# Grouped-query attention heads: two key tiles merged by predicate, four transposes a head, and value differences

## The chip, the cores and the metric

The kernel runs on one core of one Trainium2 chip. The metric is the device time of one execution in microseconds (us). Engine names follow the profile: PE is TensorE's matmuls, PEld its weight loads, DVE is VectorE, ACT is ScalarE, POOL is GpSimd, SP is the engine that issues the DMAs.

## The reference

One layer of a hybrid trunk on x of 512 tokens by 2048 channels, all float32: RMS norm, one input projection, three token mixers (A: dilated attention, 8 heads; B: a convolution module; C: sliding-window attention, 16 query heads on 2 key/value heads, 64 wide), an output projection with a residual, and a SwiGLU block with a residual. The change is in mixer C:

```python
cq = _rms_norm(cq.reshape(B, S, C_Q_HEADS, HEAD_DIM), c_q_g[l])
ck = _rms_norm(ck.reshape(B, S, C_KV_HEADS, HEAD_DIM), c_k_g[l])
cv = cv.reshape(B, S, C_KV_HEADS, HEAD_DIM)
out_c, _ = _band_attention(cq, ck, cv, C_WINDOW - 1, sinks=c_sinks[l])
```

`_band_attention` lets query t see the keys t-127 to t, takes exp(s - m), adds exp(sink - m) to the sum, multiplies by v and divides by the sum. The window is 128, so each query sees exactly 128 keys (fewer for the first 127 queries).

## The kernel before, in words

Activations lie transposed, channels on partitions and the 512 tokens as columns. Every float32 product is made of float32r parts, high and low: `mm3` (L311 to L314) issues high x high, high x low and low x high into one PSUM bank.

The program is written out in the order in which it is to run. `project` (L477) makes one 128-channel tile of the input projection by 48 matmuls 512 columns wide; after every six of them a tick is counted, and functions that are due at that tick append their instructions to the queues of their engines. `PROJ` (L47) is the order of the tiles: cv and ck early, then the q tiles of C, each with two heads, mixed with tiles for B and A. So the work of C's heads stands on PE between matmuls of the projections, and on DVE between weight splits (L290) and convolution taps (L513), from about 110 to 385 us of the span.

For one C head, `attention` (L715) cuts the 512 queries into four tiles of 128. Query tile i sees keys of tile i (the later keys, up to the diagonal) and of tile i-1 (the earlier keys, above the diagonal): a triangle of each. The steps, by `C_TICKS` (L43):

- `scores(u)`, L729: two units of two query tiles, each in one PSUM bank, 256 columns per query tile (tile 0 has 128 keys, beside which its low parts stand).
- `top(u)`, L741: DVE adds the mask bias_c to the whole 256 columns and takes the maximum, one instruction for each query tile (L750).
- `exps(u)`, L757: ACT takes the exponential of 256 columns, with the sum (L763); tile 0 has 128.
- `norm(u)`, L768: DVE makes the reciprocal of the sum, POOL multiplies the 256 columns by it (L779).
- `flip(t)`, L790: PE transposes the 128x128 blocks of the weights, seven for a head, four in the first PSUM bank and three in the second (`TBANKS`, L708).
- `high(t)` and `low(t)`, L799 and L804: ACT copies a bank to float32r (tile ph), DVE subtracts it (tile pl, L806).
- `weigh()`, L808: for each of four key tiles j, PE multiplies the values of j (high and low side by side as 128 columns) by ph and by pl: eight matmuls, six 256 wide and two 128 wide (L819, L820), into one bank, which `out_high` and `out_rows` add up.

When each step is due is worked out at the end of `attention`: `at_v` (L839) is the tick of `weigh` after that of the first scores, 18 before the change. The next head follows six ticks later. `do_v` (L679) transposes the values of the two key/value heads once, and splits them into high and low parts. `slot` (L145) takes a tile of 512 columns out of a pool of 67.

Of the kernel before, what the change touches and what calls it, by code (L numbers as in the profile page):

```python
# [15 lines left out]
P = 128  # L16
# [25 lines left out]

C_TICKS = (1, 6, 2, 2, 2, 2, 4, 1, 3)  # L43
A_TICKS = (0, 7, 2, 1, 3, 1, 3, 1, 2)
# [78 lines left out]
def kernel(ctx: ExitStack, tc: tile.TileContext, xT, wi, wo, wgu, wd, cst_in, outT):  # L123
# [253 lines left out]
    bias_a = slot("bias_a")  # L377
    bias_c = slot("bias_c", cols=2 * P)
    gqk = cp.tile([P, 2], F32, name="gqk")
# [3 lines left out]
    di2 = slot("di2", I32)  # L383
    nc.gpsimd.iota(di2[:, :2 * P], pattern=[[-1, 2 * P]], base=P, channel_multiplier=1)

    def masks():
# [9 lines left out]
        nc.vector.tensor_scalar(bias_a, mult_a, 0.0, BIG, op0=ALU.is_equal, op1=ALU.mult)  # L396
        nc.vector.tensor_copy(df[:, :2 * P], di2[:, :2 * P])
        nc.vector.tensor_scalar(r[:, :2 * P], df[:, :2 * P], 127.0, None, op0=ALU.is_le)
        nc.vector.scalar_tensor_tensor(r[:, :2 * P], df[:, :2 * P], 0.0, r[:, :2 * P], op0=ALU.is_ge, op1=ALU.mult)
        nc.vector.tensor_scalar(bias_c, r[:, :2 * P], 0.0, BIG, op0=ALU.is_equal, op1=ALU.mult)  # L400
        for i in range(2):
# [277 lines left out]
    def do_v(box, b, name):  # L679
        vs = slot(name + "s")  # L680
        nc.vector.tensor_mul(vs, b, r1b)

        def flip():
            b2 = bank(name + "t")
            for i in range(NT):
                nc.tensor.transpose(b2[:, i * P:(i + 1) * P], vs[:, i * P:(i + 1) * P], ident)
            ticks.after(1, high, b2.rearrange("p (a b c) -> p a b c", a=NT, b=2))

        def high(src):
            box["v"] = [slot(f"{name}{h}", F32R).rearrange("p (a b c) -> p a b c", a=NT, b=2) for h in range(2)]  # L690
            for h in range(2):
                nc.scalar.copy(box["v"][h][:, :, h], src[:, :, h])
            ticks.after(1, low, src)

        def low(src):
            for h, v in enumerate(box["v"]):
                nc.vector.tensor_sub(v[:, :, 1 - h], src[:, :, h], v[:, :, h].bitcast(F32))

        box["v at"] = ticks.now + VD + 3
        ticks.after(VD, flip)  # L700
# [14 lines left out]
    def attention(kind, box, mix, mi, heads):  # L715
        ready, every, step, s1, sx, s2, fl, ev, we = C_TICKS if kind == "c" else A_TICKS
        name = mi
        us = UNITS[kind]
        mask = bias_c if kind == "c" else bias_a
        mw = mask.shape[-1]  # L720
        st = {}

        def head(h):
# [17 lines left out]
            def top(u):  # L741
                b, rq = banks[u], box["rq"]
                s = slice(us[u][0][0], us[u][-1][0] + 1)
                if kind == "c" and u == 0:
                    with_kl = slot(f"kl{h}", F32, P)
                    nc.scalar.copy(with_kl, b[:, P:2 * P])
                    nc.vector.tensor_add(with_kl, with_kl, mask[:, mw - P:])
                for i, k0, n, o in reversed(us[u]):
                    other = with_kl if kind == "c" and i == 0 else mask[:, mw - n:]
                    nc.vector.tensor_tensor_reduce(b[:, o:o + n], b[:, o:o + n], other,  # L750
                                                   op0=ALU.add, op1=ALU.max, scale=1.0, scalar=-3.0e38,
                                                   accum_out=mx[:, i:i + 1])
# [4 lines left out]
            def exps(u):  # L757
                b, rq = banks.pop(u), box["rq"]
                e = es[u] = slot(f"{name}e{h}{u}")
                s = slice(us[u][0][0], us[u][-1][0] + 1)  # L760
                for i, k0, n, o in us[u]:
                    acc = dict(accum_out=den[:, i:i + 1]) if kind == "c" else {}
                    nc.scalar.activation(e[:, o:o + n], b[:, o:o + n], AF.Exp, bias=nm[:, i:i + 1],  # L763
                                         scale=rq[:, i, h:h + 1], **acc)
                if kind == "c":
                    nc.scalar.activation(mx[:, s], nm[:, s], AF.Exp, bias=col(C_SINK + heads[h]))

            def norm(u):  # L768
# [8 lines left out]
                nc.vector.reciprocal(rd[:, s], den[:, s])  # L777
                for i, k0, n, o in us[u]:
                    nc.gpsimd.tensor_scalar(e[:, o:o + n], e[:, o:o + n], rd[:, i:i + 1], None, op0=ALU.mult)  # L779

            ph, pl = {}, {}

            def block(i, j):
                for u, un in enumerate(us):
                    for ii, k0, n, o in un:
# [18 lines left out]
            def low(t, b, o):  # L804
                pl[t] = slot(f"{name}pl{h}{t}", F32R)
                nc.vector.tensor_sub(pl[t][:, :o], b[:, :o], ph[t][:, :o].bitcast(F32))  # L806

            def weigh():  # L808
                b = bank(f"{name}o{h}")
                vals = box["v"][h]  # L810
                first = True
                for t, tb in enumerate(TBANKS[kind]):
                    o = 0
# [216 lines left out]
    for half in range(2):  # L1030
# [33 lines left out]
    m_hi = m_lo = r1b = mult_a = bias_a = bias_c = None  # L1064

# [470 lines left out]
```

## Time and profile before

| | |
|---|---|
| median of 3 runs | 1879.44 us |
| the runs | 1879.31 to 1881.54 us |
| span of the profiled execution | 1877.5 us |
| instructions | 28557 |
| PE, DVE, ACT, POOL busy | 100%, 77%, 72%, 65% of the span |
| matmuls, each with a weight load | 9848 |
| granted TensorE clock | 1.00 |

The profile is of one execution of its own, whose time is shown as its span, from the first to the last instruction; the median of the runs is 1.9 us longer. In rows of the timeline stand the start, the duration, engine, line, operation, output<-inputs, the shape and, in brackets, an idle time before it and what ended it. A matmul's duration contains its way through the pipeline, so that following matmuls overlap. In rows by group stand the count, then after the bar the busy time in us and the mean of one in ns.

### The profile page before, as it was taken

How to read it: one execution, taken by the hardware profiler on the slowest of the kernel's cores; microseconds unless marked ns; L12 is line 12 of the kernel's file. 1: busy time of each engine (PE TensorE's matmuls, PEld its weight loads, DVE VectorE, ACT ScalarE, POOL GpSimd, SP SyncE). 2: the span in 40 equal slices, each digit the busy share in tenths (PEclk: the TensorE clock that was granted, in tenths of full speed). 3: DMA queues.
4: the chain of work that ended last, by engine and by line, in shares of the span. 5: the costliest groups of instructions: out<-in, count | busy, mean ns of one | idle time of the engine just before them, and what ended most of it. 6: DMA issues, size and time to landing. Idle time of an engine off the chain costs nothing.

```text
span 1877.5 us, 28557 instructions
## 1 busy us (share of the span) xinstructions
PE 1871.7 (100%) x9848; PEld 1609.1 (86%) x9848; DVE 1454.1 (77%) x2376; ACT 1343.7 (72%) x1883; POOL 1217.0 (65%) x812
## 2 busy tenths in 40 slices
PE   9999999999999999999999999999999999999999
PEld 7888888888888888888888888888888888888888
DVE  7578999897679777777777777777777677778887
ACT  6246655553466887888878888888888887777675
POOL 5023444362155887778878877888787767766786
PEclk9999999999999999999999999999999999999999
DMA  7333233333342354443544445344455475578984
GB/s 271 122 109 102 81 105 102 121 107 138 113 146 89 114 178 142 163 163 132 184 134 164 162 137 181 132 166 160 145 175 196 151 237 185 196 253 283 311 241 124
DMA packets 157986, 301.09 MB, mean 160 GB/s; under 512 B 29968, under 2 KB 69008, under 8 KB 157840
## 3 DMA queue, kind: packets, MB, share of 16 engines
q1 hardware_dynamic: 157696, 299.25, 48.8%
q8 instruction: 78, 1.28, 0.3%
q14 instruction: 68, 0.56, 0.1%
q10 hardware_dynamic: 144, 0.01, 0.0%
HBM read 241.27 MB, written 50.33 MB: 155 GB/s over the span
## 4 chain that ended last, share of the span: by engine, by line
PE 96%; DVE 1%; issue 1%; ACT 1%; POOL 1%; DMA 0%; SPq 0%; DVEq 0%; POOLq 0%; ACTq 0%
PE out L1125 51%; PE out L1267 16%; PE o L313 3%; PE o L314 3%; PE o L312 3%; PE cq L312 1%; PE cq L313 1%; PE cq L314 1%; PE in L313 1%; PE ak L312 1%; PE bg L312 1%; PE ak L314 1%; PE ak L313 1%; PE bu L312 1%; PE bu L314 1%; PE bg L313 1%
## 5 line engine op out<-in xcount | busy, mean ns | idle before, releaser
L1125 PE MATMUL out<-h,wh 128*128 128x512 f32 x2464 | 588.4, 391 | 0.0
L1125 PEld LDWEIGHTS out<-h,wh 128*128 128x128 f32 x2464 | 452.7, 188 | 87.5
L1125 PEld LDWEIGHTS out<-h,wl 128*128 128x128 f32 x2464 | 316.2, 191 | 12.4 <-DVE wl L295 0.4
L1125 PE MATMUL out<-h,wl 128*128 128x256 f32 x2464 | 320.3, 283 | 0.2 <-DVE wl L295 0.2
L1267 PE MATMUL out<-wh,a 128*128 128x512 f32 x896 | 221.3, 389 | 0.0
L1267 PEld LDWEIGHTS out<-wh,a 128*128 128x128 f32 x896 | 168.2, 188 | 34.9
L289 ACT CAST wh<-w 128x1024 fp32r<-128x1024 f32 (+1 forms) x93 | 96.7, 1042 | 125.0 <-PE o L313 43.3
L290 DVE TENSOR_TENSOR wl<-w,wh 128x1024 fp32r<-128x1024 f32 (+1 forms) x93 | 117.2, 1262 | 46.7 <-ACT wh L289 45.7
L1267 PE MATMUL out<-wl,a 128*128 128x512 f32 x448 | 119.7, 389 | 0.0
L1267 PEld LDWEIGHTS out<-wl,a 128*128 128x128 f32 x448 | 84.1, 188 | 17.4
L513 DVE SCALAR_TENSOR_TENSOR y<-bu,cst,y 128x511 f32<-128x511 f32 (+14 forms) x120 | 90.3, 753 | 0.7
L1125 PE MATMUL out<-a,wh 128*128 128x512 f32 x330 | 80.1, 391 | 0.0
L1125 PEld LDWEIGHTS out<-a,wh 128*128 128x128 f32 x330 | 60.2, 188 | 11.4
L312 PE MATMUL o<-mh_c,wh 128*128 128x512 f32 x128 | 51.2, 400 | 0.0
L313 PE MATMUL o<-ml_c,wh 128*128 128x512 f32 x128 | 50.1, 392 | 0.4 <-POOL ml_c L865 0.3
L314 PE MATMUL o<-mh_c,wl 128*128 128x512 f32 x128 | 50.1, 391 | 0.0
L1312 DVE TENSOR_TENSOR Y<-Y,out 128x512 f32<-128x512 f32 x48 | 30.8, 683 | 19.0 <-PE out L1267 18.9
L1125 PEld LDWEIGHTS out<-a,wl 128*128 128x128 f32 x330 | 43.3, 191 | 2.2
L1125 PE MATMUL out<-a,wl 128*128 128x256 f32 x330 | 44.0, 283 | 0.0
L429 POOL TENSOR_TENSOR ssum<-ssum,sq 128x512 f32<-128x512 f32 x15 | 26.6, 1770 | 19.3 <-ACT sq L428 18.8
L312 PE MATMUL cq<-hh,wh 128*128 128x512 f32 x96 | 38.6, 402 | 0.0
L314 PE MATMUL cq<-hh,wl 128*128 128x512 f32 x96 | 37.5, 391 | 0.0
(3111 smaller groups left out, 5197.0 us busy)
## 6 DMA issues: line engine op xcount, KB each, us to landing
od<-a SPq DMA_DIRECT2D x140, 256.0 KB, 4.7
a<-od SPq DMA_DIRECT2D x140, 256.0 KB, 6.2
w<-in_wi SPq DMA_DIRECT2D x59, 512.0 KB, 3.6
w<-in_wo SPq DMA_DIRECT2D x32, 512.0 KB, 3.6
x<-in_xT SPq DMA_DIRECT2D x16, 256.0 KB, 6.7
xr<-in_xT SPq DMA_DIRECT2D x16, 256.0 KB, 3.8
x2d<-xr SPq DMA_DIRECT2D x16, 256.0 KB, 2.0
yd<-z SPq DMA_DIRECT2D x16, 256.0 KB, 5.5
```

The costliest lines, as they stand in the source:

```text
L289: nc.scalar.copy(hi[:, :n], t[:, :n])
L290: eng.tensor_sub(lo[:, :n], t[:, :n], hi[:, :n].bitcast(F32))
L312: nc.tensor.matmul(out, wh, xh, start=start, stop=False)
L313: nc.tensor.matmul(out, wh, xl, start=False, stop=False)
L314: nc.tensor.matmul(out, wl, xh, start=False, stop=stop)
L429: eng.tensor_add(acc, acc, sq)
L513: nc.vector.scalar_tensor_tensor(yconv[j][:, i:], hconv[j][:, :T - i], c, yconv[j][:, i:], op0=ALU.mult, op1=ALU.add)
L1125: nc.tensor.matmul(out, lhs[:, s], rhs, start=begin, stop=last and low == flip[0] and x is xs[-1], skip_group_check=True)
L1267: nc.tensor.matmul(to[h], x[:, h * P:(h + 1) * P], v[:, j], start=sub == 0 and h not in started, stop=sub == 1 and n in (len(todo) - 1, le ...
L1312: nc.vector.tensor_add(t, t, b)
```

## The change

Since the two triangles of a query tile together are exactly 128 keys, they fit into one block: column k of the block holds the score of the later key where k is at most the query's place in the tile, and that of the earlier key elsewhere.

- `top` lays the earlier key's score over the later one's with a predicated copy on DVE (mask `earlier`, int32), one for each unit, and takes the maximum of the 128 columns with `tensor_reduce`. Query tile 0, which has no earlier tile, keeps the old way, with bias_c as a 128-column mask.
- `exps` takes 128 columns of every query tile, and all four go into one tile e; `norm` multiplies 128 columns each.
- `flip` transposes four blocks, in one bank; `high` and `low` run once a head.
- `weigh` uses p for all of a query tile's 128 keys times v of tile i, plus p of the earlier keys alone times (v of tile i-1 less v of tile i). For that `low` has POOL multiply ph and pl, 384 columns each, by the mask `later_keys` (tiles phb, plb), and `do_v` makes the differences of v (`step`, split to high and low parts, tiles cvd) once. The weighing is 4 + 4 + 3 + 3 = 14 matmuls, each 128 wide.
- The last number of `C_TICKS` goes from 3 to 5. With one bank of transposes in place of two, `at_v` goes from 18 to 19.

```diff
-C_TICKS = (1, 6, 2, 2, 2, 2, 4, 1, 3)
+C_TICKS = (1, 6, 2, 2, 2, 2, 4, 1, 5)
...
+        nc.vector.tensor_scalar(later_keys, df[:, :3 * P], 0.0, None, op0=ALU.is_gt)
+        nc.vector.tensor_scalar(bias_c, df[:, 3 * P:], 0.0, BIG, op0=ALU.is_lt, op1=ALU.mult)
+        nc.vector.tensor_scalar(earlier[:, :2 * P], df[:, :2 * P], 0.0, None, op0=ALU.is_lt)
...
+            full = slot(name + "w").rearrange("p (a b c) -> p a b c", a=NT, b=2)
+            nc.scalar.copy(full, src)
...
+            step = slot(name + "d").rearrange("p (a b c) -> p a b c", a=NT, b=2)
+            nc.vector.tensor_sub(step[:, 1:], full[:, :NT - 1], src[:, 1:])
+            ticks.after(1, step_high, step)
...
-        "c": [[(0, 0, 1), (1, 1, 2)], [(2, 2, 3), (3, 3, 3)]],
+        "c": [[(i, i, i) for i in range(NT)]],
...
+                if grouped:
+                    first = 1 - u
+                    pair = b.rearrange("p (i t k) -> p i t k", i=2, t=2)[:, first:]
+                    keys = earlier[:, :2 * P].rearrange("p (i k) -> p i k", i=2)[:, first:]
+                    nc.vector.copy_predicated(pair[:, :, 1], keys, pair[:, :, 0])
+                    nc.vector.tensor_reduce(mx[:, 2 * u + first:2 * u + 2], pair[:, :, 1],
+                                            axis=mybir.AxisListType.X, op=ALU.max)
...
+                    if grouped:
+                        src, to = b[:, o + n - P:o + n], e[:, i * P:(i + 1) * P]
...
+                if grouped:
+                    for part, p in (("h", ph), ("l", pl)):
+                        p["before"] = slot(f"{name}p{part}b{h}", F32R)
+                        nc.gpsimd.tensor_mul(p["before"][:, P:], p[t][:, P:].bitcast(F32), later_keys)
...
+                if grouped:
+                    todo = [(v, i, p[k]) for v, k, i0 in ((vals, 0, 0), (box["dv"][h], "before", 1))
+                            for p in (ph, pl) for i in range(i0, NT)]
+                    for n, (v, i, p) in enumerate(todo):
+                        s = slice(i * P, (i + 1) * P)
+                        nc.tensor.matmul(b[:, s], v[:, i].rearrange("p a b -> p (a b)"), p[:, s], start=n == 0,
+                                         stop=n == len(todo) - 1, skip_group_check=True)
```

The first place is on PE, at the weighing of the first head of c3 (c3o), before. The rows follow the projection's matmuls (cq); c3t are transposes of the second head of c3, c1s scores of c1.

```order
L314 MATMUL cq_1491<-hh_384,wl_1420 128x512
L819 MATMUL c3o_1576<-c3ph_1509,cv_831 128x256
L820 MATMUL c3o_1576<-c3pl_1527,cv_831 128x256
...
L819 MATMUL c3o_1576<-c3ph_1524,cv_831 128x128
L820 MATMUL c3o_1576<-c3pl_1541,cv_831 128x128
L795 MATMUL c3t_1585<-ident,c3e_1441 128x128 x3
L795 MATMUL c3t_1585<-ident,c3e_1481 128x128
L736 MATMUL c1s_1590<-ck_1039,cq_1487 128x256
```

The same place on PE in the changed kernel; cvd are the differences of v, phb and plb the products by `later_keys`.

```order
L314 MATMUL cq_1491<-hh_385,wl_1431 128x512
L826 MATMUL c3t_1587<-ident,c3e_1451 128x128 x4
L752 MATMUL c1s_1592<-ck_1050,cq_1487 128x256
...
L314 MATMUL cq_1491<-hh_429,wl_1431 128x512
L852 MATMUL c3o_1606<-c3ph_1519,cv_832 128x128 x4
L852 MATMUL c3o_1606<-c3pl_1535,cv_832 128x128 x4
L852 MATMUL c3o_1606<-c3phb_1537,cvd_856 128x128 x3
L852 MATMUL c3o_1606<-c3plb_1539,cvd_856 128x128 x3
L312 MATMUL cq_1491<-hh_448,wh_1430 128x512
```

The weighing has moved six projection matmuls (one tick) behind the transposes of the next head, has 14 narrow matmuls in place of eight, and the second group of transposes is gone.

The second place is POOL's queue from the second head of c0 to q of c1 (cq1r, a power), before; c3e are the weights of the two heads of c3, which are normalised here, bu is a product of mixer B.

```order
L504 TENSOR_TENSOR bu_1211<-bu_1211,bg_1340 128x512
L779 TENSOR_SCALAR c3e_1319<-c3e_1319,c3d_1062 128x128
L779 TENSOR_SCALAR c3e_1319<-c3e_1319,c3d_1062 128x256
L779 TENSOR_SCALAR c3e_1369<-c3e_1369,c3d_1062 128x256 x2
L779 TENSOR_SCALAR c3e_1441<-c3e_1441,c3d_1063 128x128
L779 TENSOR_SCALAR c3e_1441<-c3e_1441,c3d_1063 128x256
L779 TENSOR_SCALAR c3e_1481<-c3e_1481,c3d_1063 128x256 x2
L585 TENSOR_TENSOR cq1r<-cq1v,nhalf 128x8
```

The same stretch of POOL's queue in the changed kernel:

```order
L506 TENSOR_TENSOR bu_1223<-bu_1223,bg_1348 128x512
L808 TENSOR_SCALAR c3e_1327<-c3e_1327,c3d_1073 128x128 x4
L841 TENSOR_TENSOR c0phb_1426<-c0ph_1396,mask_c 128x384
L841 TENSOR_TENSOR c0plb_1428<-c0pl_1424,mask_c 128x384
L808 TENSOR_SCALAR c3e_1451<-c3e_1451,c3d_1074 128x128 x4
L841 TENSOR_TENSOR c3phb_1537<-c3ph_1519,mask_c 128x384
L841 TENSOR_TENSOR c3plb_1539<-c3pl_1535,mask_c 128x384
L587 TENSOR_TENSOR cq1r<-cq1v,nhalf 128x8
```

Two products stand in the queue for each head, behind the normalisation of the following head.

More of the change, by code (lines that the diff above doesn't have):

```diff
@@ L718, in attention @@
         us = UNITS[kind]
-        mask = bias_c if kind == "c" else bias_a
-        mw = mask.shape[-1]
+        grouped = kind == "c"
         st = {}
@@ L743, in top @@
                 s = slice(us[u][0][0], us[u][-1][0] + 1)
-                if kind == "c" and u == 0:
+                if grouped and u == 0:
                     with_kl = slot(f"kl{h}", F32, P)
                     nc.scalar.copy(with_kl, b[:, P:2 * P])
-                    nc.vector.tensor_add(with_kl, with_kl, mask[:, mw - P:])
+                    nc.vector.tensor_add(with_kl, with_kl, bias_c)
+                if grouped:
[5 more added lines that the diff above has]
+                                            axis=mybir.AxisListType.X, op=ALU.max)
                 for i, k0, n, o in reversed(us[u]):
-                    other = with_kl if kind == "c" and i == 0 else mask[:, mw - n:]
+                    if grouped and i:
+                        continue
+                    other = with_kl if grouped else bias_a[:, T - n:]
                     nc.vector.tensor_tensor_reduce(b[:, o:o + n], b[:, o:o + n], other,
```

41 lines of the change are left out of this document (27 added, 14 removed).

## Prediction

> **What bounds the kernel now.** I read the page first (shares, chain), then TensorE's waits, then the busy time of each engine in two stretches of the stage that is changed, and last the timeline of TensorE around single groups of matmuls. The page:
>
> ```profile
> span 1877.5 us, 28557 instructions
> ...
> PE 1871.7 (100%) x9848; PEld 1609.1 (86%) x9848; DVE 1454.1 (77%) x2376; ACT 1343.7 (72%) x1883; POOL 1217.0 (65%) x812
> ...
> PE 96%; DVE 1%; issue 1%; ACT 1%; POOL 1%; DMA 0%; SPq 0%; DVEq 0%; POOLq 0%; ACTq 0%
> ```
>
> TensorE is busy all the time and holds 96% of the chain that ended last. Its waits, by what it waited for:
>
> ```profile
> PE idle L409 <- DVE bones L343: 1.4, 1, 1.4
> PE o L313 <- POOL ml_c L865: 0.3, 1, 0.3
> PE c0o L820 <- DVE c0pl L806: 0.2, 1, 0.2
> ```
>
> Under a microsecond of waits lies behind the warm-up, and one of them, at c0o, is in code that changes. So two things alone can move the time: what TensorE itself has to do, and a new wait. Columns of the next rows: the stretch, its sum, then PE, PEld, DVE, ACT and POOL busy, granted clock, DMA share.
>
> ```profile
> 140.00:180.00 40.00, 39.76 (x214) 33.84 (x213) 35.48 (x88) 24.26 (x56) 12.37 (x13) 1.00 0.32 96
> 180.00:220.00 40.00, 40.00 (x212) 34.05 (x211) 37.72 (x101) 24.18 (x56) 20.77 (x19) 1.00 0.36 101
> ```
>
> The clock is granted in full. VectorE is the second engine: (40 - 35.48) + (40 - 37.72) = 6.8 us free of 80, or 8.5%. ScalarE and GpSimd have room.
>
> **What a matmul costs TensorE.** A row's duration includes the pipeline, so I use distances from start to start. One weighing (o = v x weights) of the kernel before, between projections:
>
> ```profile
> 309.42 0.39 PE L313 MATMUL bg<-hl,wh 128*128 128x512 f32 x1
> 309.64 0.39 PE L314 MATMUL bg<-hh,wl 128*128 128x512 f32 x1
> 309.87 0.28 PE L819 MATMUL c4o<-c4ph,cv 128*128 128x256 f32 x1
> ...
> 310.46 0.28 PE L820 MATMUL c4o<-c4pl,cv 128*128 128x256 f32 x1
> 310.58 0.22 PE L819 MATMUL c4o<-c4ph,cv 128*128 128x128 f32 x1
> 310.64 0.28 PE L820 MATMUL c4o<-c4pl,cv 128*128 128x128 f32 x1
> 310.76 0.45 PE L312 MATMUL bg<-hh,wh 128*128 128x512 f32 x1
> 311.04 0.39 PE L313 MATMUL bg<-hl,wh 128*128 128x512 f32 x1
> ```
>
> A 512-wide matmul takes 0.23 us (309.64 to 309.87). From 309.64 to 311.04 are 1.40 us; less two 512-wide ones (L314 and L312, 0.46) the eight matmuls of the weighing cost 0.94. Six are 256 wide: 309.87 to 310.58 is 0.71, 0.12 each. The two 128-wide ones are left with 0.94 - 0.71 = 0.23, so 0.115 each: as much as 256 columns, though the first of them is followed after 0.06. The weight loads of the same place say why:
>
> ```profile
> 310.47 0.19 PEld L819 LDWEIGHTS c4o<-c4ph,cv 128*128 128x128 f32 x1
> 310.59 0.19 PEld L820 LDWEIGHTS c4o<-c4pl,cv 128*128 128x128 f32 x1
> 310.70 0.19 PEld L312 LDWEIGHTS bg<-hh,wh 128*128 128x128 f32 x1
> 310.81 0.19 PEld L313 LDWEIGHTS bg<-hl,wh 128*128 128x128 f32 x1
> ```
>
> Every matmul has a load of its own, and they start no closer than 0.11 us, behind the 128-wide matmuls too. A matmul narrower than about 256 columns costs its load. Transposes agree:
>
> ```profile
> 160.05 0.39 PE L314 MATMUL cq<-h,wl 128*128 128x512 f32 x1
> 160.28 0.49 PE L795 MATMUL c3t<-ident,c3e 128*128 128x128 f32 x3
> 160.53 0.48 PE L312 MATMUL cq<-h,wh 128*128 128x512 f32 x1
> 160.84 0.39 PE L313 MATMUL cq<-h,wh 128*128 128x512 f32 x1
> ```
>
> 160.05 to 160.84 less 0.46 is 0.33 for three, 0.11 each.
>
> **The change on TensorE.** The order of instructions shows that it does what it says: transposes of the grouped heads fall from 112 to 64 (7 to 4 for each of 16 heads), weighing matmuls rise from 128 to 224 (8 to 14), all 128 wide, and no other matmul changes.
> - Transposes: 3 x 0.11 = 0.33 us less a head.
> - Weighing: 14 x 0.112 (between the 0.11 of the loads and the 0.115 of the pair) = 1.57 against 0.94: 0.63 more a head. With 0.11 it is 0.60, with 0.115 0.67. The columns that stream are the same, 14 x 128 = 1,792; what grows is the number of weight loads.
> - Sum: +0.30 a head (0.27 to 0.34), 16 heads: **+4.8 us** (4.3 to 5.4). It all lies on the path, since TensorE has no idle time to hide it.
>
> Here a rule of the Trainium skill speaks the other way. Its page "TensorE: Matmul & The Clock Gate", section "Back-to-back issue gap", gives about 81 ns sustained for a matmul of 128 columns with its load. By that figure a weighing would be 14 x 0.081 = 1.13, +0.19 a head, and the sum (0.19 - 0.33) x 16 = -2.2 us, faster. The same section's 131 ns for 512 columns is not what this trace has (0.23), so I hold to the rows.
>
> **The wait at c0o.** In the second head of c0 TensorE stood still for the second tile of low parts:
>
> ```profile
> 157.40 0.28 PE L820 MATMUL c0o<-c0pl,cv 128*128 128x256 f32 x1
> 157.52 0.28 PE L819 MATMUL c0o<-c0ph,cv 128*128 128x256 f32 x1
> 158.03 0.39 PE L820 MATMUL c0o<-c0pl,cv 128*128 128x256 f32 x1 [0.24 <-DVE c0pl L806]
> ```
>
> 0.51 instead of 0.12: 0.39 lost. After the change the second tile is gone and the weighing stands one tick later, so this goes: **-0.4 us**. In all 4.8 - 0.4 = +4.4.
>
> **The new wait.** The weighing now needs two products by GpSimd (high and low parts by the mask of later keys). Behind a weighing that waits all of TensorE waits, the projection's matmuls queued after it. What is free there, at the tightest first head, c3:
>
> ```profile
> 164.65 1.83 POOL L779 TENSOR_SCALAR c3e<-c3e,c3d 128x256 f32<-128x256 f32 x2 [1.91 <-DVE c3d L777]
> 165.15 0.69 DVE L806 TENSOR_TENSOR c3pl<-c3t,c3ph 128x512 fp32r<-128x512 f32 x1
> 167.91 0.28 PE L819 MATMUL c3o<-c3ph,cv 128*128 128x256 f32 x1
> ```
>
> In GpSimd's queue the products of this head stand behind the normalisation of the next one, which ended at 166.48; the low parts were ready at 165.84. A product of 384 columns is not in the trace. Bounds for it, with the other prices, by group (busy, then mean ns):
>
> ```profile
> L504 POOL TENSOR_TENSOR bu<-bu,bg 128x512 f32<-128x512 f32 x3 | 3.9, 1287 | 9.6 <-ACT bg L503 9.6
> L779 POOL TENSOR_SCALAR c3e<-c3e,c3d 128x256 f32<-128x256 f32 x6 | 5.6, 942 | 1.9 <-DVE c3d L777 1.9
> L779 POOL TENSOR_SCALAR c3e<-c3e,c3d 128x128 f32<-128x128 f32 x2 | 1.6, 808 | 6.9 <-DVE c3d L777 6.9
> L750 DVE CUSTOM_DVE_ANT_0 c3s<-c3s,bias_c 128x256 f32<-128x256 f32 x6 | 2.5, 425 | 0.1
> L750 DVE CUSTOM_DVE_ANT_0 c3s<-c3s,kl 128x128 f32<-128x128 f32 x2 | 0.6, 298 | 0.1
> L806 DVE TENSOR_TENSOR c3pl<-c3t,c3ph 128x384 fp32r<-128x384 f32 x1 | 0.5, 543 | 0.0
> ```
>
> A 512-wide product took 1.29, so one of 384 columns takes 0.97 (by width) to 1.29; I take 0.97. Both are done by 166.48 + 2.6 = 169.1 at the latest. The weighing starts at 167.91 plus one tick of six 512-wide matmuls (6 x 0.23 = 1.4): 169.3, and it reads the first product only as its ninth matmul, 8 x 0.112 = 0.9 later. So 1.1 us are left in the worst case, and I cost the wait at nothing; if GpSimd comes 2 us later than I work out, every head would wait about 0.9, 14 us in all.
>
> **The other engines.** VectorE loses the 384-wide subtraction (0.54 a head). Three 256-wide add-and-max give way to two predicated copies and two maxima, one of each 128 and one 256 wide. A predicated copy and a plain maximum are not in the trace; by the nearest rows (0.43 for 256, 0.30 for 128) the four cost 1.45 against 3 x 0.43 = 1.28 and the accumulator readings that follow those, so about level; at double price a copy pair costs 0.7 more. ScalarE exponentiates four times 128 columns where one 128 and three 256 stood, and copies one tile less. GpSimd saves 3 x (0.942 - 0.808) = 0.4 a head and gains 2 x 0.97. All this is off the path while VectorE has its 8.5%. Differences of v and the masks are made once, before the first head; the like step for v took
>
> ```profile
> 92.44 0.75 DVE L697 TENSOR_TENSOR cv<-cvt,cv 128x256 fp32r<-128x256 f32 x2
> ```
>
> and two or three of these lie beside projections: nothing, or 2 us once if they were uncovered.
>
> **Rivals.** *GpSimd holds VectorE up (slower still).* There is a sign of it:
>
> ```profile
> 148.33 0.71 DVE L513 SCALAR_TENSOR_TENSOR y<-bu,cst,y 128x483 f32<-128x483 f32 x1
> 149.16 1.28 POOL L504 TENSOR_TENSOR bu<-bu,bg 128x512 f32<-128x512 f32 x1 [5.75 <-ACT bg L503]
> 149.23 1.73 DVE L513 SCALAR_TENSOR_TENSOR y<-bu,cst,y 128x482 f32<-128x482 f32 x1
> ```
>
> The convolution tap that began just behind GpSimd's product took 1.73 instead of 0.71. If each of the 32 new products cost VectorE its whole length, that is 1.94 a head against 0.54 saved: 1.4 more. Two weighings in a row, c0's second (157.40 less three matmuls of 0.12) and c3's first (167.91), lie 10.9 us apart, 8.5% of which is 0.92: the point from which it decides. VectorE would fall 0.5 a head behind, 16 x 0.5 = 8 us at most, and the low parts would come late: 1879.4 + 4.4 + 4 (half) = **1888**. Against it: many of VectorE's operations read PSUM, and a lag must first use up the 1.1 us above. The Trainium skill has the rule on its page "SBUF — State Buffer", section "Who interferes with whom": a VectorE instruction with two SBUF inputs and a GpSimd instruction that reads SBUF exclude each other for a whole instruction; the row at 149.23 agrees.
>
> *Loads hide behind narrow matmuls (faster).* If a run of 128-wide matmuls went at the 0.06 that lies between 310.58 and 310.64, a weighing would take 14 x 0.06 = 0.84, 0.10 less than now, and the change would give (0.10 + 0.33) x 16 + 0.4 = 7.3 us: **1872**. It decides below (0.94 + 0.33) / 14 = 0.091 us a matmul. For it: only pairs of such matmuls stand in the trace, no run of 14. Against it: loads and transposes hold 0.11 wherever they follow each other. The Trainium skill's 81 ns, above, would be this rival in part.
>
> **How the numbers follow.** The profiled span, 1877.5, becomes 1881.9; 1.9 us lie around it up to the median of the runs, 1879.44, so the forecast is 1883.8. Chances: the forecast 0.80, GpSimd and VectorE 0.13, hidden loads 0.07. What a measurement of this kernel can tell from no change is about 0.2%, 3.8 us. The forecast's own range is 1882.7 to 1886.5: at the low end 4.3 - 0.4 = 3.9 less 0.6 for the scatter of a median, at the high end 5.4 and up to 1.7 of small waits. About a fifth of its chance lies under 3.8. So slower 0.76 (0.63 and the first rival), same 0.17, faster 0.07. The range reaches to the first rival's 1888 and on the other side to a load cost somewhat under the rows: 1881.0 to 1888.0.
>
> **What would show it.** Right: c-transposes four to a group at 0.11; fourteen weighing matmuls in about 1.57 us with loads 0.11 apart; TensorE still at 100% with no wait at L852; VectorE a little less busy in 140 to 220. Wrong: matmul starts at 0.06 to 0.08 within a weighing (faster), or waits of TensorE on the products (phb, plb) or on pl, with taps of over 1 us beside the products (slower still).

## The result, and the profile after

The changed kernel takes **1889.09 us** (median of 5 runs, 1888.53 to 1890.65), the kernel before 1879.44 in the same session (5 runs, 1878.97 to 1881.54). The ratio is 1.0053, 95% interval 1.0041 to 1.0065: slower by 9.65 us. The forecast was 1883.8 with a range up to 1888.0, so the sign was right and the size was not: +4.4 was forecast, about twice that came. One execution each of e2_we4 (7361 us) and e9_tri6 (5035 us), two kernels of the experiments, ran several times slower than the others of the same kernel and is left out.

The page of the changed kernel, the three lines that were shown of before:

```profile
span 1888.7 us, 28672 instructions
...
PE 1879.2 (99%) x9896; PEld 1616.2 (86%) x9896; DVE 1460.6 (77%) x2331; ACT 1331.7 (71%) x1870; POOL 1242.4 (66%) x844
...
PE 93%; DVE 4%; ACT 1%; DMA 1%; issue 1%; POOL 1%; SPq 0%; DVEq 0%; ACTq 0%; POOLq 0%
```

TensorE has 48 matmuls more, as worked out (96 of the weighing more, 48 transposes less). But its share of the chain fell from 96% to 93%, and VectorE and DMA now stand in it. Its waits say where (us in total, times, longest):

```profile
PE o L313 <- POOL ml_c L909: 1.3, 2, 0.9
PE a0s L755 <- DVE ak0l L654: 1.1, 1, 1.1
PE c7s L752 <- DMA cq<-cq7lo: 0.8, 1, 0.8
PE c1s L752 <- DMA cq<-cq1lo: 0.7, 1, 0.7
PE in L312 <- ACT wh L289: 0.6, 1, 0.6
PE a1s L755 <- DVE ak1l L654: 0.3, 1, 0.3
```

No weighing waits: L852 does not appear, and c0o's wait is gone. What waits are the **scores** of later heads (c1s, c7s, a0s, a1s), whose code on TensorE the change hardly touched, and the output projection (o). The weighing itself, in one stretch of TensorE's timeline:

```profile
172.47 0.39 PE L314 MATMUL cq<-hh,wl 128*128 128x512 f32 x1
172.70 0.56 PE L852 MATMUL c3o<-c3ph,cv 128*128 128x128 f32 x4
173.09 0.61 PE L852 MATMUL c3o<-c3pl,cv 128*128 128x128 f32 x4
173.54 0.50 PE L852 MATMUL c3o<-c3phb,cvd 128*128 128x128 f32 x3
173.87 0.50 PE L852 MATMUL c3o<-c3plb,cvd 128*128 128x128 f32 x3
174.21 0.44 PE L312 MATMUL cq<-hh,wh 128*128 128x512 f32 x1
174.49 0.40 PE L313 MATMUL cq<-hl,wh 128*128 128x512 f32 x1
```

From 172.47 to 174.49 are 2.02 us; less two 512-wide matmuls (0.46) the fourteen cost 1.56, or 0.111 each; 1.57 was forecast. The busy time in the two stretches (PE, PEld, DVE, ACT, POOL, clock, DMA share):

```profile
140.00:180.00 40.00, 39.26 (x210) 33.40 (x209) 35.99 (x70) 21.42 (x49) 20.39 (x22) 1.00 0.26 79
180.00:220.00 40.00, 40.00 (x222) 34.52 (x221) 37.65 (x92) 20.11 (x55) 22.10 (x23) 1.00 0.37 106
```

GpSimd has 20.39 and 22.10 where it had 12.37 and 20.77. VectorE has fewer instructions (70 and 92 for 88 and 101) but the same busy time (73.64 of 80 against 73.20), where the prediction's signs had it a little less busy. VectorE's timeline, and GpSimd's in the same stretch:

```profile
168.51 1.24 DVE L515 SCALAR_TENSOR_TENSOR y<-bu,cst,y 128x508 f32<-128x508 f32 x1
169.68 2.01 DVE L290 TENSOR_TENSOR wl<-w,wh 128x1024 fp32r<-128x1024 f32 x1
171.62 0.73 DVE L515 SCALAR_TENSOR_TENSOR y<-bu,cst,y 128x507 f32<-128x507 f32 x1
```
```profile
168.20 1.01 POOL L841 TENSOR_TENSOR c3phb<-c3ph,mask_c 128x384 fp32r<-128x384 f32 x1
169.17 1.44 POOL L841 TENSOR_TENSOR c3plb<-c3pl,mask_c 128x384 fp32r<-128x384 f32 x1
```

The convolution tap (128x508) that began beside a product took 1.24, the next (128x507), clear of both, 0.73. The weight split between them took 2.01; an undisturbed one of this width takes 1.2 (a row of 1.21 stands in the experiments). So the products seem to hold VectorE, which the experiments test. Of the first rival's signs, taps of over 1 us are there, waits at the weighing are not.

Start to start on TensorE, the two spans compare so: its own work +4.3; lost at c1s 0.9, c7s 1.0, a0s 1.3, a1s 0.5 and 0.9 more at ml_c, less 0.4 at c0o and 0.3 at a transposition of mixer A that no longer waits, +3.9; small gaps +1.2; and 1.8 more before 11 us, where the first weights came later in the profiled run (the slowest of its five). I don't count the last to the change: runs of one kernel lie over 2 us apart. Without it the parts make 9.4.

### The profile page after: what moved, and what is told of

Its sections match the earlier page's. It is cut to its first block, busy times and chain, and to the rows that moved or that the text cites. A ratio compares the mean times of both kernels' runs of the same rounds, so it can differ in the third digit from the quotient of the medians.

```text
span 1888.7 us, 28672 instructions
## 1 busy us (share of the span) xinstructions
PE 1879.2 (99%) x9896; PEld 1616.2 (86%) x9896; DVE 1460.6 (77%) x2331; ACT 1331.7 (71%) x1870; POOL 1242.4 (66%) x844
## 4 chain that ended last, share of the span: by engine, by line
PE 93%; DVE 4%; ACT 1%; DMA 1%; issue 1%; POOL 1%; SPq 0%; DVEq 0%; ACTq 0%; POOLq 0%
PE out L1169 51%; PE out L1311 16%; PE o L313 3%; PE o L314 3%; PE o L312 3%; PE cq L312 1%; PE cq L314 1%; PE cq L313 1%; DVE wl L290 1%; PE in L313 1%; PE in L312 1%; PE in L314 1%; PE bu L312 1%; PE bu L313 1%; PE bu L314 1%
## 5 line engine op out<-in xcount | busy, mean ns | idle before, releaser
L515 DVE SCALAR_TENSOR_TENSOR y<-bu,cst,y 128x511 f32<-128x511 f32 (+14 forms) x120 | 98.3, 819 | 0.9
```

The source lines that it names most:

```text
L515: nc.vector.scalar_tensor_tensor(yconv[j][:, i:], hconv[j][:, :T - i], c, yconv[j][:, i:], op0=ALU.mult, op1=ALU.add)
```

## The experiments

Three theories for the part that was not forecast. **Loads:** narrow matmuls cost more than I took. **Tick:** the weighing moved one tick later, from ahead of the next head's transposes and scores to behind them; 0.94 us of work that covered those scores is gone, and their inputs, which came just in time, are late. **Port:** products with two SBUF operands on GpSimd hold VectorE, whose small steps feed everything else. Each run stands beside the kernel before on the same chip; differences in us are between the two medians. The intervals given are some 2 us wide to each side. A difference of 3 us between two of these runs therefore rests on more: their single times don't overlap, and the kernel before has the same median within 0.5 us on every chip.

**1. The loads alone.** The kernel before with its weighing cut to 128 columns, 14 matmuls a head:

```diff
-                        nc.tensor.matmul(out, v, ph[t][:, o:o + n], start=first, stop=False, skip_group_check=True)
-                        nc.tensor.matmul(out, v, pl[t][:, o:o + n], start=False, stop=last, skip_group_check=True)
-                        first = False
+                        cuts = range(0, n, P if kind == "c" else n)
+                        for part in (ph, pl):
+                            for c in cuts:
+                                m = P if kind == "c" else n
+                                nc.tensor.matmul(out[:, c:c + m], v, part[t][:, o + c:o + c + m], start=first,
+                                                 stop=last and part is pl and c == cuts[-1], skip_group_check=True)
+                                first = False
```

> The kernel before, with each 256-wide matmul of C's weighing cut into two of 128 columns: 14 narrow matmuls a head from the same tiles, seven transposes as before, nothing else. If a narrow matmul costs its weight load (0.112 us), a weighing takes 1.57 instead of 0.94 us: 16 x 0.63 = 10.1, about 1889.5. If loads hide behind a run of narrow matmuls at 0.06, 1878; at 0.081, 1882.

Measured 1889.63 (+10.4, ratio 1.0054, interval 1.0039 to 1.0069). Of TensorE's waits behind the start, these are all:

```profile
PE o L313 <- POOL ml_c L869: 0.3, 1, 0.3
PE in L313 <- DVE wl L290: 0.2, 1, 0.2
PE out L1129 <- DVE wl L295: 0.2, 1, 0.2
```

So this is pure work: 10.4 / 16 = 0.65 a head, where 0.63 was forecast. The loads theory explains the forecast, not the miss, and loads don't hide behind narrow matmuls.

**2. The tick.** The changed kernel with its weighing at the old tick, 18, and the kernel before with its weighing at 19:

```diff
-C_TICKS = (1, 6, 2, 2, 2, 2, 4, 1, 5)
+C_TICKS = (1, 6, 2, 2, 2, 2, 4, 1, 4)
```
```diff
-C_TICKS = (1, 6, 2, 2, 2, 2, 4, 1, 3)
+C_TICKS = (1, 6, 2, 2, 2, 2, 4, 1, 4)
```

The first is e2_we4 and e2b_we4, the second e4_late.

> The changed kernel with the last number of C_TICKS at 4, so that the weighing stands at the tick where it stood before (18 after the first scores), ahead of the next scores. Arrival theory (TensorE comes to the scores too early because the weighing moved behind them): the waits at c1s, a0s and a1s go, 0.9 + 1.3 + 0.5, about 1886.5. Port theory (GpSimd's products hold VectorE up, which is late with q, k and the rest): the same waits stay, 1889 within 0.5.

> The kernel before with its weighing one tick later (19 after the first scores), nothing else. Arrival theory: waits of up to 0.9 us each appear at the scores of c1, a0 and a1, and the one at c0o (0.4) goes: 1880.5 to 1882. Port theory: no waits appear and c0o's goes: 1879.0.

> The run with the weighing at its old tick once more, for its trace: what waits of TensorE are left between 1886.0 and 1883.7. Port theory: waits at scores or in the late ml_c products of under 1 us each, 2.3 in all, behind VectorE operations that a product held up.

e2_we4: 1885.87 (+6.6; 1.0035, 1.0022 to 1.0047), 3.1 less than the changed kernel's 9.65; e2b_we4, a single run, 1885.81. The trace of e2b_we4 has 1.1 at c7s, 0.3 at ml_c as in the kernel before, and 0.3 and 0.2 at the weighings of c5 and c0, which wait there for a product (plb); no scores of c1, a0 or a1 wait. So at the old tick the products do come slightly late: the later tick avoids 0.5 us of waits and costs some 3. e4_late: 1882.24 (+3.0; 1.0016, 1.0006 to 1.0025). Its longest waits on TensorE:

```profile
PE o L313 <- POOL ml_c L865: 1.2, 2, 0.9
PE c7s L736 <- DMA cq<-cq7lo: 1.0, 1, 1.0
PE a0s L739 <- DVE ak0l L652: 0.6, 1, 0.6
```

This is the kernel before, with not one instruction added: the waits at c7s, a0s and ml_c come from the tick, and the tick is a cause by itself. Waits at the scores of c1 and a1, which were expected too, did not come; those at c7s and ml_c were not expected. They come by more than one way.

- **a0s** has lost its cover: the weighing c4o stood ahead of the first scores of a0 and now stands behind them. Every trace with the weighing at the later tick shows a wait at a0s (0.2 to 2.4), and none with it at the old tick.
- **c7s** has not: the weighing c5o is ahead of it in both orders. Here the input is late. TensorE started c7s at 239.29 in the kernel before and could have at 238.58 in e4_late; VectorE began its low parts of q (cq7lo) 5.35 us ahead of that in the kernel before and 3.24 in e4_late, 2.1 less. 0.8 of it is there at the end of a step of mixer B on VectorE (bg, L502) already. 1.3 come on ScalarE, where an ACT_TABLE_LOAD stands between the exponentials and mixer B's activation: it ran ahead of the wait for bg in the kernel before (first pair of rows) and runs behind it in e4_late (second pair). Why it changed its place is not known. It stands behind in e1_narrow and e6_select4 too, where c7s does not wait, so it is not enough alone.
- **ml_c**, low parts of C's output, is read by the output projection, where no weighing stands. How the tick makes it late was not worked out.

```profile
216.06 1.28 ACT L503 ACT_TABLE_LOAD   x1
218.40 0.63 ACT L503 ACTIVATE bg<-bg 128x512 f32<-128x512 f32 x1 [1.06 <-DVE bg L502]
```
```profile
218.52 1.28 ACT L503 ACT_TABLE_LOAD   x1 [3.24 <-DVE bg L502]
219.82 0.63 ACT L503 ACTIVATE bg<-bg 128x512 f32<-128x512 f32 x1
```

**3. The port.** The changed kernel without its products (the weighing reads ph and pl in their place, so the mask of the later keys is left out):

```diff
-                    for part, p in (("h", ph), ("l", pl)):
-                        p["before"] = slot(f"{name}p{part}b{h}", F32R)
-                        nc.gpsimd.tensor_mul(p["before"][:, P:], p[t][:, P:].bitcast(F32), later_keys)
+                    for p in (ph, pl):
+                        p["before"] = p[t]
```

> The changed kernel without GpSimd's two products: the weighing reads ph and pl in their place (so the mask of later keys is left out and the output is another), with the same 14 matmuls. Port theory: all four waits (c1s, c7s, a0s, a1s) go, 1889.1 less 3.7 = about 1885.4. Arrival theory: only the wait at c7s goes, since c1s, a0s and a1s come from TensorE's order: about 1888.

Measured 1885.48 (+6.2; 1.0034, 1.0019 to 1.0048), 3.5 less than the changed kernel's 9.65. Then the same tiles made by an affine select on GpSimd, which reads one operand from SBUF where the product reads two:

```diff
-                        nc.gpsimd.tensor_mul(p["before"][:, P:], p[t][:, P:].bitcast(F32), later_keys)
+                        nc.gpsimd.affine_select(out=p["before"][:, P:], in_=p[t][:, P:].bitcast(F32),
+                                                pattern=[[0, NT - 1], [-1, P]], base=0, channel_multiplier=1,
+                                                compare_op=ALU.is_gt, fill=0.0)
```

> The changed kernel, with GpSimd's two products by a mask tile written as two affine selects, which read one SBUF operand in place of two, at the same ticks and with the same result. If a product holds VectorE up because it has two SBUF operands: as without products, 1885.5, and VectorE's taps beside the selects keep 0.7 us. If any GpSimd instruction that reads SBUF does so, or if it is the place in GpSimd's queue: 1889, as the changed kernel.

Measured 1885.89 (+6.8; 1.0038, 1.0023 to 1.0053): as good as no products. The taps tell why; the line of the 120 taps in the changed kernel's page, then in that of e6b_select5 (after the bar the sum in us and the mean in ns):

```profile
L515 DVE SCALAR_TENSOR_TENSOR y<-bu,cst,y 128x511 f32<-128x511 f32 (+14 forms) x120 | 98.3, 819 | 0.9
```
```profile
L515 DVE SCALAR_TENSOR_TENSOR y<-bu,cst,y 128x511 f32<-128x511 f32 (+14 forms) x120 | 92.3, 769 | 0.9
```

That is 6 us of VectorE's time on the taps alone; over the whole span VectorE is busy for 1460.6 us in the changed kernel and for 1448.9 in e6b_select5, with as many instructions. And to the kernel before, two spare products a head were added that nothing reads, 384 columns wide (e10_prodonly); e13_selonly has selects in their place:

```diff
                 nc.vector.tensor_sub(pl[t][:, :o], b[:, :o], ph[t][:, :o].bitcast(F32))
+                if kind == "c" and t == 1:
+                    for part, p in (("h", ph), ("l", pl)):
+                        spare = slot(f"{name}p{part}b{h}", F32R)
+                        nc.gpsimd.tensor_mul(spare[:, :3 * P], p[t][:, :3 * P].bitcast(F32), bias_a[:, :3 * P])
```

> The kernel before, with two spare products a grouped-query head on GpSimd (two SBUF operands, 384 columns, of the second bank's high and low parts), which nothing reads. TensorE's work and order are those of before. If such products hold VectorE's instructions and this reaches the scores also where the weighing has not moved, 1880.5 to 1882.5; if they hurt only because the weighing's move has used up the slack, 1879.0 to 1880.0 and TensorE's waits as in before.

> The kernel before with the two spare products written as affine selects, which read one SBUF operand. If two-operand products hurt by holding VectorE, 1879 to 1880.5. If they hurt because GpSimd itself has more to do (its other steps come later), as the products: 1883 to 1885.

e10_prodonly: 1884.94 (+5.3; 1.0029, 1.0018 to 1.0040), more than either theory gave. e13_selonly: 1880.82 (+1.6; 1.0009, 0.9999 to 1.0018), hardly to be told from no change, though 0.3 above what the port alone allows; c0o still waits for 0.8 there. It takes as many tiles out of the pool as e10_prodonly, so tiles are not what the products cost. TensorE's waits in e10_prodonly:

```profile
PE c0o L824 <- DVE c0pl L806: 1.5, 2, 1.3
...
PE c7s L736 <- DMA cq<-cq7lo: 1.0, 1, 1.0
PE o L313 <- POOL ml_c L869: 1.0, 2, 0.6
```

And how a product reaches c0o, in VectorE's timeline and in GpSimd's:

```profile
155.32 0.97 DVE L753 SCALAR_TENSOR_TENSOR c3d<-c3d,cq3r 128x2 f32<-128x2 f32 x1
...
157.66 1.21 DVE L290 TENSOR_TENSOR wl<-w,wh 128x1024 fp32r<-128x1024 f32 x1
...
159.25 0.54 DVE L806 TENSOR_TENSOR c0pl<-c0t,c0ph 128x384 fp32r<-128x384 f32 x1
```
```profile
155.26 1.01 POOL L810 TENSOR_TENSOR c0phb<-c0ph,bias_a 128x384 fp32r<-128x384 f32 x1
```

An instruction on two columns took 0.97, until the product was done (156.27). In the kernel before the same one took 0.16:

```profile
154.32 0.16 DVE L753 SCALAR_TENSOR_TENSOR c3d<-c3d,cq3r 128x2 f32<-128x2 f32 x1
```

The low parts of c0 stand behind it in VectorE's queue, and c0o waited for them: 1.3 at the second tile of low parts, where the kernel before waits for 0.24. The Trainium skill, "SBUF — State Buffer", section "Who interferes with whom", says that a VectorE instruction with two SBUF inputs contends with a GpSimd instruction that reads SBUF, and calls their shared port pair an exclusive lock. The trace agrees for the product: the step ended 0.02 us after it. A select reads SBUF too, and would contend by the same rule; yet beside selects VectorE loses little (sums below, under the hardware), and e6b_select5 and e13_selonly decide what that is worth.

A select is also shorter than a product (0.52 at best against 1.01), so part of what it saves may lie in GpSimd's own queue. But the waits that go with it in the changed kernel (c1s, c7s, a1s and half of a0s) were for VectorE and for the DMAs of q, none for GpSimd.

**4. Neither, and both.** No products at the old tick (e5_pure; the mask of the later keys is left out here too); selects at the old tick, the changed kernel with both causes out and all else kept (e6_select4); and the kernel before with both causes put in (e12_prodlate).

Each joins two edits that are shown above: e5_pure those of e3_noprod and e2_we4, e6_select4 those of e6b_select5 and e2_we4, e12_prodlate those of e10_prodonly and e4_late. In all three the line is now

```diff
+C_TICKS = (1, 6, 2, 2, 2, 2, 4, 1, 4)
```

> The changed kernel with both causes away: no products by GpSimd (the mask of later keys is left out, the output is another) and the last number of C_TICKS at 4. If the two causes are all there is, the prediction's TensorE term stands alone: 1879.3 + 4.8 less the wait at c0o (0.4) = 1883.7, and no wait of over 0.4 us at scores, in C or A. If something else of the change (predicated copies, slots) makes it wait: 1885 or more.

> The changed kernel with both causes taken out, and the rest kept: affine selects in place of the products, and the weighing at its old tick. If the two causes are all that stands above TensorE's own extra work, 1883.7 to 1884.7, as the kernel without products at the old tick (1884.2). If something else of GpSimd's work counts, over 1885.2.

> The kernel before with both: the two spare products a head (alone +5.3 us) and the weighing one tick later (alone +3.0 us). If the two hurt at different places, their sum, 1887 to 1888.5. If they hold up the same chain of scores and TensorE pays the later of the two, 1884 to 1886, as in the changed kernel, where both together stand 5.7 us above the same kernel with neither.

e5_pure: 1884.21 (+5.1; 1.0027, 1.0016 to 1.0038). e6_select4: **1883.41** (+3.8; 1.0019, 1.0010 to 1.0028), 0.3 under what was expected and 0.4 under the prediction's 1883.8. Its waits on TensorE:

```profile
PE in L312 <- ACT wh L289: 0.6, 1, 0.6
PE o L313 <- POOL ml_c L911: 0.3, 1, 0.3
```

All waits at scores are gone and ml_c is back at 0.3: this is the kernel that I forecast. e12_prodlate: 1885.54 (+6.3; 1.0035, 1.0024 to 1.0047), with waits of 2.1 at a0s, 1.3 at c1s and 0.6 each at c7s and a1s: the scores of the changed kernel's list, in the kernel before. The time lies in the range of the second case. In a table, us above the kernel before:

| | neither | tick alone | products alone | both |
|---|---|---|---|---|
| changed kernel (selects where it has no products) | 3.8 | 6.8 | 6.6 | 9.65 |
| kernel before | 0 | 3.0 | 5.3 | 6.3 |

In the changed kernel the two add up (3.8 + 3.0 + 2.8 = 9.6). In the kernel before the sum is 2.0 too large (3.0 + 5.3 against 6.3), which the intervals don't settle; the traces speak for it, since its weighing at the old tick also waits for low parts (c0o 1.5 in e10_prodonly), and that wait is gone with the later tick. By place, among these runs, the waits at c1s and a1s stand only where the tick and the products come together (the changed kernel, e12_prodlate); a0s needs the tick; c7s comes with the products alone (e2b_we4, e10_prodonly) or, in the kernel before, with the tick alone.

The prices are less firm than the table looks. With no products at all the tick is worth 1.1 (from e5_pure, +5.1, to e3_noprod, +6.2), and products at the old tick then cost 1.5 (e5_pure to e2_we4). Why e5_pure, which has less to do, stands at +5.1 where e6_select4 is at +3.8 is open; the intervals overlap, and its only waits are two of 1 us at transposes of mixer A.

**5. The same idea without either cause.** Four transposes a head, each transposed bank copied into both triangles, zeroed by eight affine selects a head, and the eight wide matmuls of before: 48 transposes less, no matmul more, 16 x 0.33 = 5.3 us less for TensorE.

```diff
+            def triangles(two):
+                for t, n in zip(two, (2, 1)):
+                    at = t.rearrange("p (a t k) -> p a t k", a=2, t=2)
+                    for c, m, sign, op in ((0, 2, -1, ALU.is_ge), (1, n, 1, ALU.is_gt)):
+                        part = at[:, :m, c]
+                        nc.gpsimd.affine_select(out=part, in_=part.bitcast(F32), pattern=[[0, m], [-sign, P]], base=0,
+                                                channel_multiplier=sign, compare_op=op, fill=0.0)
...
+                    triangles(ph[t])
+                    triangles(pl[t])
```

The last number of C_TICKS is 4 in e7_tri (the weighing at its old tick), 5 in e8_tri5, 6 in e9_tri6. e14_tri_early and e15_tri_early6 have the transposes one tick earlier (the number before the last two 3 in place of 4) and 5 and 6 at the end, so that the weighing stands at the old tick and one later. e11_tri_act is e7_tri with ScalarE in GpSimd's place for the normalisation:

```diff
+                        nc.scalar.activation(e[:, o:o + n], e[:, o:o + n], AF.Copy, scale=rd[:, i:i + 1])
```

> An attempt to keep the four transposes and give the narrow matmuls up: after the transposes each block is copied twice, one copy keeps the later keys and one the earlier keys (affine selects by GpSimd, in place), and they lie so that the weighing is the eight wide matmuls of before; no products, no differences of v; the last number of C_TICKS is 4. TensorE then loses only the transposes: 1879.3 - 16 x 0.33 - 0.4 = 1873.6. If GpSimd's eight selects a head (some 3.5 us) come late, waits at the weighing eat it: 1880 or more.

> The kernel with four transposes a head and the triangles made by affine selects (e7_tri), with its weighing one tick later. TensorE's own work is 5.3 us less than before. If its waits at the weighing (some 9 us for selects) go with that one tick and the later weighing costs its 3 us, 1877 to 1880. If GpSimd's queue is behind by more than a tick, waits on selects stay and it is 1882 to 1888.

> The same with the weighing two ticks later. If one tick more lets the selects come in time, as e8_tri5 or up to 2 us faster (1876 to 1879). If the later weighing costs its own waits each time, 2 to 4 us slower than e8_tri5.

> The kernel with four transposes a head and triangles by affine selects, the weighing at its old tick, and the blocks' normalisation moved from GpSimd to ScalarE (four multiplications a head). If only GpSimd's late selects held the weighing, 1874 to 1876.5, ahead of both kernels. If ScalarE now comes late with the copies that the scores wait for, 1877 to 1884.

> The kernel with four transposes a head and affine-select triangles (e7_tri), its transposes, copies and selects one tick earlier and the weighing at its old tick, where the scores find their inputs. If the blocks are normalised in time for the earlier transposes, the waits for selects (some 9 us in e7_tri) go and it is 1874 to 1878, ahead of the kernel before. If the transposes now wait for GpSimd's normalisation, 1880 to 1886.

> The same with the weighing one tick later than before. As e8_tri5 less its waits for selects: 1879 to 1883, its scores waiting as there, and slower than e14_tri_early by 2 to 5 us if the weighing's tick alone is what the scores pay for.

None beats the kernel before; e11_tri_act, e14_tri_early and e15_tri_early6 came out above all their cases, and e9_tri6, 5.5 us under e8_tri5, in neither of its two. e7_tri 1888.80 (1.0053, 1.0037 to 1.0070), e8_tri5 1885.99 (1.0031, 1.0019 to 1.0044), e9_tri6 1880.54 (1.0005, 0.9995 to 1.0014: no difference that can be measured), e14_tri_early 1890.97 (1.0063, 1.0046 to 1.0080), e15_tri_early6 1892.84 (1.0077, 1.0062 to 1.0092), e11_tri_act 1931.85 (1.0280, 1.0265 to 1.0295). One tick of delay for the weighing moves most of the waits from selects at the weighing (e7_tri, first list) to the scores (e8_tri5, second, which keeps 2.0 at selects), and an earlier transposition meets the normalisation (e14_tri_early, third). e9_tri6 has no trace that can be compared.

```profile
PE c1o L857 <- POOL c1pl1y L834: 1.4, 1, 1.4
PE c0o L857 <- POOL c0pl1x L834: 0.9, 1, 0.9
```
```profile
PE a0s L740 <- DVE ak0l L654: 2.4, 1, 2.4
...
PE c1s L737 <- DMA cq<-cq1lo: 0.8, 1, 0.8
```
```profile
PE c2t L811 <- POOL c2e L793: 3.6, 2, 3.2
PE c3t L811 <- POOL c3e L793: 3.4, 3, 2.7
```

So GpSimd's steps have no whole tick to spare at either end in these runs. e11_tri_act missed by most: ScalarE's normalisation stands in its queue ahead of the next exponentials and waits for VectorE's reciprocal.

```profile
161.32 0.29 ACT L779 ACTIVATE c3d<-c3d,cst 128x2 f32<-128x2 f32 x1
167.50 0.70 ACT L794 ACTIVATE c3e<-c3e,c3d 128x128 f32<-128x128 f32 x2 [5.88 <-DVE c3d L790]
168.10 0.44 ACT L777 ACTIVATE c3e<-c3s,c3d,cq3r 128x128 f32<-128x128 f32 x1
```

ScalarE, busy half of this stage in the changed kernel (21.42 of 40), stood still for 5.88 with exponentials and the copy of q behind the waiting step. The mean granted clock there was 0.989, which over 1929 us is some 21 us of clock, by estimate up to two fifths of the +53; the last section shows how such a loss begins. All that was forecast here was 1874 to 1884.

## Why the prediction was wrong, step by step

- **What bounds the kernel** held: TensorE's work and its waits alone moved the time.
- **The change on TensorE** held: 0.111 us a narrow matmul (0.112 taken), 1.56 a weighing (1.57), and e6_select4, without new waits, at +3.8 for a forecast of +4.4. The Trainium skill's 81 ns at 128 columns ("TensorE: Matmul & The Clock Gate", section "Back-to-back issue gap"), which would have made the change faster, is not what this chip did in float32r with a load for each matmul: 0.111 us here.
- **The wait at c0o** went, as said. But the same move was counted as a gain only. This is one step that failed: the prediction said that "the weighing stands one tick later, so this goes" and did not ask what stood behind the weighing in TensorE's queue. The order of instructions showed it: c1s follows c3o at the old place and precedes it at the new one. Scores that had 0.94 us of weighing ahead of them lost that cover (c1s, a0s, a1s). That is not all of the price: of the 3.0 us of e4_late, 0.6 were waited at a0s, 1.0 at c7s and 0.9 more at ml_c, and these last two are inputs that came late from other engines, with no weighing gone from ahead of them. Price: 3.0 (e4_late) to 3.1 us (e2_we4 against the changed kernel), but 1.1 without products.
- **The new wait** was costed at nothing at the weighing, and at the weighing there was none, by the later tick. The product's price (0.97 taken) was 1.01 where it ran clear of others and up to 1.79 on the average of a pair.
- **The other engines** is the other step that failed: "All this is off the path while VectorE has its 8.5%." The share is an average; the path runs through single small steps (maximum, scale, copy of q, DMA of q, scores), and one of them held for a product's length is late by that length, whatever is free afterwards. The row of 0.97 in e10_prodonly shows it at c0o; at the scores it is argued from the waits that go. Price: 2.8 (e6_select4 to e2_we4) to 3.5 (e3_noprod to the changed kernel), but 1.5 from e5_pure.
- **First rival** (GpSimd holds VectorE up, 1888, chance 0.13): its mechanism is shown and its price, 4, was near; it should have been the forecast's own term, since the row at 149.23 already showed a tap held for a second microsecond. Its reckoning was wrong in two places: it decides at the first held step on a chain without slack, not at 0.92 us a head, and in the changed kernel it shows at the scores, not at the low parts. With the rival's 4 and the tick's 3 the forecast would have been 1883.8 + 7 = 1890.8.
- **Second rival** (hidden loads) fell with e1_narrow.

What is only argued: that the DMAs of q (c1s, c7s) were late because the copies ahead of them were; the profile of the changed kernel shows a step on two columns behind the maximum held until a product ended ahead of c7's copy, and the waits vanish with the products and the tick, but no run delayed that copy alone, and in e4_late, which has no products, the same wait came by another way. Part of that way, the ACT_TABLE_LOAD behind the wait for bg, is in the changed kernel's trace too (223.57, after 3.71 of waiting).

## What to carry to other kernels

When a step is moved in an engine's queue, list what it stood ahead of: it may have been the cover of the next operation's inputs, and a kernel whose bound engine never waits may be on that edge in many places at once. Then list what follows from the step on the other engines, since that moves too. Before work is given to an engine that can hold up another, look for the smallest instructions of the other engine that lie on a chain without slack, not for its average share of free time. And write a mask on GpSimd as an affine select with one operand, not as a product with a mask tile: here that was worth 3 us at the changed kernel's own tick.

## What the runs showed of the hardware

**Products and selects beside VectorE.** For each VectorE instruction that overlaps one of these GpSimd instructions by over 0.1 us I took its duration less the median of the same line and shape. Beside the 32 products of the changed kernel the sum is 15.2 us over 71 overlaps, 23 of them of over 0.3 us; beside the 32 selects of e6b_select5 it is 3.9 us over 55, with one. A select of 384 columns took 0.52 at best, half a product; beside VectorE it is the select that stretches (group of the high parts of c2, mean ns):

```profile
L841 POOL TENSOR_SCALAR_AFFINE_SELECT c2phb<-c2ph 128x384 fp32r<-128x384 f32 x2 | 2.5, 1269 | 1.9 <-ACT c2ph L832 1.9
```

**A wait can cost TensorE more than its length.** In e7_tri the weighing of c0 and the scores around it were broken up by waits for selects; three stretches of the windows view (PE, PEld, DVE, ACT, POOL busy, granted clock, DMA share), and two rows of TensorE's timeline:

```profile
158.00:162.00 4.00, 1.86 (x11) 1.47 (x12) 3.83 (x10) 1.74 (x7) 3.20 (x8) 0.97 0.40 131
162.00:166.00 4.00, 4.00 (x14) 3.26 (x14) 3.12 (x7) 3.04 (x7) 3.00 (x4) 0.60 0.21 36
166.00:170.00 4.00, 4.00 (x21) 3.37 (x20) 2.52 (x6) 0.87 (x1) 3.71 (x8) 1.00 0.62 191
```
```profile
163.28 0.63 PE L314 MATMUL cq<-h,wl 128*128 128x512 f32 x1
163.71 0.63 PE L312 MATMUL cq<-h,wh 128*128 128x512 f32 x1
```

After 4 us in which TensorE was busy for 1.86, the mean granted clock of the next four was 0.60; in slices of 1 us it is 0.50 from 162 to 165 and 0.91 in the next. 512-wide matmuls stood 0.43 us apart in place of 0.23, though nothing waited any more. Six of them, from 162.28 to 164.99, took 2.71 us in place of 1.36, so 1.3 us came on top of the waits, and at 166 the clock was whole again. The Trainium skill's "TensorE: Matmul & The Clock Gate", section "What's actually happening", has the clock halved after an idle window of some 3.4 us. The trace agrees on the half, but here it fell after a stretch in which TensorE was busy for nearly half of the time. In the changed kernel no wait of this stage (up to 1.3 us, alone) had that effect.
